# Residual turns by plain transposes, an unshared residual tail, an earlier start of each recurrence, and fewer GpSimd clears in a two-layer hybrid decoder step

## The chip, the cores and the metric

The kernel is one program on one core of a Trainium2 chip. The metric is device time in microseconds (us), lower is better. Three runs of the kernel before gave 1719.68, 1722.98 and 1724.67 us; the median, 1722.98 us, is the time before. A profile of one more execution gives the rows quoted below. The engines of a core are TensorE (PE in the rows, with PEld for its weight loads), VectorE (DVE), ScalarE (ACT), GpSimd (POOL) and the DMA queues, of which this kernel uses SyncE's (SP).

## What is computed

A prompt of 1024 tokens and eight short samples (8 x 4 tokens) go through two layers of width 1024: a sliding-window attention layer and a gated DeltaNet layer. Cut to what matters here:

```python
for layer in range(2):
    h, gate = modulate(x, c, norm_g[layer], w_mod[layer], b_mod[layer])   # rms_norm(x) * (1 + scale) + shift
    x = x + gate * branch(h)                                              # attention, then DeltaNet
y = rms_norm(x, final_norm_g)

def gated_delta_chunked(...):
    lower = where(strict, (kb @ k.T) * decay, 0)              # one system per chunk and head
    sol = triangular_solve(lower + eye, rhs)                  # unit lower triangular
    def step(S, xs):                                          # the recurrence over the chunks
        u = w_v - w_k @ S
        o = q_dec @ S + qk @ u
        S = S * g_tot + k_dec.T @ u
        return S, o
```

Between the layers each token row is scaled by its reciprocal root mean square, turned (tokens on partitions become features on partitions) and shifted and scaled, to be the moving operand of the second layer's projections.

## The kernel before

All matrix work is in float32 accuracy: a projection splits both operands into a high and a low float32r half and adds three products (`h2hi` by `wh`, `h2lo` by `wh`, `h2hi` by `wl`). The work runs in this order: modulation and the first layer's projections; attention; the first output projection with the residual and the turn into the second layer (about 425 to 570 us of the profile); the second layer's projections with the DeltaNet work woven in (about 540 to 1436 us); the second output projection with the samples' states and the final norm (to the end).

The order on each engine is not written out by hand. The big projections (`project`, lines 549 to 574) and output products (lines 1437 to 1469) are plain loops, and between any two of their matmuls `stages()` (line 497) asks a list of generators whether their next piece may be issued. A generator yields conditions: counters of other pieces, `ready(...)` and `idle(...)`, which compare a simple clock kept by `Core` with the time at which a tile is expected, and `bank(tag)`, which hands out PSUM banks. The numbers in `K` and `KR` rank the generators. So an edit of a condition or of an operation shifts everything behind it, on all engines. Each engine then executes its own list strictly in that order. Where a helper records an operation, the profile gives it line 89.

Residual tail. `rows_in` (1328) loads a 128-token row block of `x` into one of two `xt` tiles. `add_out` (1337) multiplies the output product by the gate into a tile `y` (two buffers), adds it to one half of `xt` on GpSimd and squares it on ScalarE; the second half (`hf` = 1) of block i waits until block i-1 has left `shape` (line 1341, counter `shaped`). `shape` (1376) takes the reciprocal root (`rsqrt`, eleven small VectorE operations), makes a diagonal matrix `dg` of it, which lies in one of the two `y` buffers, and multiplies: four float32 matmuls `dg` by `xt` in each of two halves (`kk`) scale and turn the block at once into a `lg` bank. Then `fu` is shifted and scaled from the bank, and split into `h2hi` and `h2lo`. Blocks are taken in the order 0, the samples, 1 to 7, so step i = 8 is block 7. Behind the last output products stand the conv weights' transpose `cwr`, copied by VectorE to `cT`, and the first projection of the second layer (`kw`).

DeltaNet. Per pair of heads `hq` (0 to 7), `solve` (1832) makes the systems in four tiles `UZ` (one for two chunks), and sends their 32x32 diagonal blocks out by DMA. `invert` (1882) fetches them as `X`, inverts them on VectorE, and before that clears the 16 diagonal strips of the `UZ` tiles on GpSimd (lines 1892 to 1896). `diagonal` multiplies each `UZ` tile by the inverted blocks `Xd` into `M`, and then overwrites the whole `UZ` tile with the transposed inverses; `blocks` fills the parts off the diagonal in six steps. `chain` (1985) is the recurrence over eight chunks; it waits until all four tiles of its head pair are solved (`st["ready"]` = 3 counts the solve as 2 and the scores `decayed` as 1). `gating` (1992) normalizes its output with a reciprocal root on GpSimd. After the last projection (`z15`) the program waits for the solve of `hq` = 7 (2175), closes its pools and opens those of the second output projection, whose rows `of` come by DMA.

Of the kernel before, what the change touches and what calls it, by code (L numbers as in the profile page):

```python
# [5 lines left out]
F32 = mybir.dt.float32  # L6
# [8 lines left out]
P = 128  # L15
# [204 lines left out]
def body(tc, I, O, cst_ap, dbg=None):  # L220
# [27 lines left out]
        z10 z11 k6 v5 q6 z12 z13 k7 v6 q7 v7 z14 z15""".split()]  # L248
    MM = (0, 20)
    ORDER = [("q", 2), ("q", 3), ("q", 4), ("q", 5), ("z", 0), ("k", 1), ("z", 1), ("z", 2), ("q", 6), ("q", 7),  # L250
             ("z", 3), ("z", 4), ("z", 5), ("z", 6), ("z", 7)]
# [269 lines left out]
    def ready(*ts):  # L521
        return lambda: plain() or nc.ready(ts) <= nc.free["tensor"]
# [789 lines left out]
    if True:  # L1312
# [15 lines left out]
        def rows_in(i, t):  # L1328
            yield lambda: shaped[0] >= i - 1
            xt = rows_[i] = x2.tile([P, D], F32, tag="xt", name="xt", bufs=2)  # L1330
            nc.sync.dma_start(xt[0:P if t < NB else TS], xp_rows[t * P:(t + 1) * P] if t < NB else xs_rows)
            if t == NB:
                o, w = COFF["sels"]
                selt = rows_["sel"] = xo.tile([P, w], F32, name="sels")
                nc.sync.dma_start(selt, cst_ap[:, o:o + w])

        def add_out(pj, i, t, hf):

            parts = P if t < NB else TS
            ns = slice(hf * 512, (hf + 1) * 512)  # L1340
            yield lambda: gathered[0] == 2 * i + hf and i in rows_ and shaped[0] >= i - 1 + hf
            xt = rows_[i][0:parts]
# [33 lines left out]
        def shape(i, t, xt, ss, parts):  # L1376
# [7 lines left out]
            rsqrt(nc, sm, rs, sv, 1, parts)  # L1384
            dg = x2.tile([P, 512], F32, tag="y", name="dg", bufs=2)[0:parts, 0:parts]
            nc.vector.tensor_scalar_mul(dg, ident[0:parts, 0:parts], rs)
            for kk in range(2):
                yield ready(dg, xt)
                pt = yield from bank("lg")
                for q in range(4):  # L1390
                    nc.tensor.matmul(pt[:, q * parts:(q + 1) * parts], xt[:, (4 * kk + q) * P:(4 * kk + q + 1) * P], dg,
                                     start=True, stop=True)
                fu = x2.tile([P, 4, P], F32, tag="fu", name="fu", bufs=2)
# [249 lines left out]
    if True:  # L1643
# [238 lines left out]
        def invert(hq, st, Ld, Xdd):  # L1882
# [8 lines left out]
            nc.gpsimd.memset(X.rearrange("p i c -> p (i c)")[:, 0:1024:33], 1.0)  # L1891
            for cp_ in range(4):
                uv = UZ[cp_].rearrange("p h c i -> p (h c) i")
                for b in range(4):
                    bs = slice(32 * b, 32 * b + 32)
                    nc.gpsimd.memset(uv[bs, :, bs], 0.0)
            yield soon(X)
# [38 lines left out]
            def blocks():  # L1936


                for v in range(6):
# [15 lines left out]
                    st["pairs"] = max(0, v - 1)  # L1955
                st["ready"] = st.get("ready", 0) + 2
                solved[0] += 1
# [4 lines left out]
        def decayed(hq, st):  # L1962
# [8 lines left out]
            for c4 in range(2):  # L1971
# [739 lines left out]
```

## Time and profile before

| | |
|---|---|
| median of three runs | 1722.98 us (1719.68 to 1724.67) |
| the profiled execution, its own time | 1721.68 us |
| its span in the profile | 1719.9 us |
| PE busy share, idle | 95%, 90.9 us |
| DVE, ACT, POOL busy share | 70%, 50%, 36% |
| mean granted TensorE clock | 0.981 |

How to read the rows: a row of the timeline has the start and the duration in us, then engine, line, operation, the tile written, `<-`, the tiles read, shapes, and `xN` for N instructions merged; a bracket says how long the engine had idled before it and which instruction ended that wait. A row of `windows` has the stretch, then the busy time of PE, PEld, DVE, ACT and POOL in it with instruction counts, the granted TensorE clock (1.00 is full speed), the DMA share and GB/s. A float32 matmul is two instructions in the timeline, a transpose one.

### The profile page before, as it was taken

What the parts mean: (1) busy time and instruction counts of PE and PEld (TensorE: products, weight loads), DVE (VectorE), ACT (ScalarE), POOL (GpSimd) and SP (SyncE); (2) the same over time, 40 slices, a digit from 0 to 9 for tenths busy, and PEclk for the clock granted to TensorE, in tenths of its full rate; (3) what the DMA queues carried; (4) which work ended last, traced back from release to release, by engine and by line L of the source; (5) the groups of instructions that cost most, each with busy time, mean ns of one, the idle gap of its engine ahead of it and who ended that gap; (6) DMA issues with size and microseconds to landing.
All of it is one profiled execution on the core that took longest, in us unless ns stands there. A gap on an engine that the chain in (4) does not pass through costs nothing.

```text
span 1719.9 us, 31798 instructions
## 1 busy us (share of the span) xinstructions
PE 1629.0 (95%) x10666; PEld 1436.5 (84%) x10666; DVE 1204.6 (70%) x3538; ACT 862.6 (50%) x2514; POOL 613.4 (36%) x1170
## 2 busy tenths in 40 slices
PE   6999999998999999999899999999999998999897
PEld 5988888986777898999889899899999896767685
DVE  4526676564565578897889878788797875468677
ACT  4625565444333546475463655654656654333332
POOL 2601111112112226463453534445344455323332
PEclk9999999999999999999999999999999999999999
DMA  9542221233243142232332324224242237765885
GB/s 331 150 138 66 59 58 50 56 89 111 86 134 105 54 111 50 66 97 56 106 74 66 98 52 112 64 72 114 51 115 60 51 85 209 236 181 160 255 259 171
DMA packets 281573, 191.78 MB, mean 112 GB/s; under 512 B 98361, under 2 KB 253881, under 8 KB 281378
## 3 DMA queue, kind: packets, MB, share of 16 engines
q1 hardware_dynamic: 281410, 189.75, 38.1%
q8 instruction: 85, 1.39, 0.3%
q14 instruction: 78, 0.64, 0.1%
HBM read 144.68 MB, written 47.04 MB: 111 GB/s over the span
## 4 chain that ended last, share of the span: by engine, by line
PE 30%; DVE 8%; DMA 4%; ACT 3%; issue 2%; POOL 2%; SPq 1%; POOLq 0%; ACTq 0%; DVEq 0%
PE ps_pj L89 17%; PE ps_lg L89 4%; PE ps_mi L89 4%; PE ps_tr L89 2%; PE ps_ob L89 2%; DMA S<-in_state_gdn_s 2%; DVE vT L89 1%; DVE UZ L89 1%; DMA out_new_s_s<-S 1%; POOL rst L89 1%; DMA out_y_p<-xt 1%; DVE rst L89 1%; DVE S L89 1%; SPq L89 1%; DVE tmp L89 0%
## 5 line engine op out<-in xcount | busy, mean ns | idle before, releaser
L89 PE MATMUL ps_pj<-h2hi,wl 128*128 128x384 f32 (+1 forms) x1128 | 383.1, 340 | 2.7 <-POOL wl L89 2.7
L89 PE MATMUL ps_pj<-h2hi,wh 128*128 128x384 f32 (+1 forms) x1128 | 383.2, 340 | 2.1 <-ACT wh L89 2.1
L89 PE MATMUL ps_pj<-h2lo,wh 128*128 128x384 f32 (+1 forms) x1128 | 381.6, 338 | 0.0
L89 POOL TENSOR_TENSOR wl<-wr,wh 128x512 fp32r<-128x512 f32 x122 | 163.4, 1340 | 543.3 <-ACT wh L89 492.9
L89 PEld LDWEIGHTS ps_pj<-h2hi,wl 128*128 128x128 f32 x1128 | 216.0, 191 | 6.8 <-POOL wl L89 3.6
L89 PEld LDWEIGHTS ps_pj<-h2hi,wh 128*128 128x128 f32 x1128 | 215.9, 191 | 4.8 <-ACT wh L89 2.4
L89 PEld LDWEIGHTS ps_pj<-h2lo,wh 128*128 128x128 f32 x1128 | 215.7, 191 | 3.3
L89 POOL TENSOR_TENSOR xt<-xt,y 128x512 f32<-128x512 f32 (+1 forms) x48 | 64.0, 1337 | 173.5 <-DVE y L89 138.1
L89 PE MATMUL ps_pj<-hlo,wh 128*128 128x384 f32 (+1 forms) x360 | 119.0, 331 | 0.0
L89 PE MATMUL ps_pj<-hhi,wh 128*128 128x384 f32 (+1 forms) x360 | 118.4, 329 | 0.0
L89 PE MATMUL ps_pj<-hhi,wl 128*128 128x384 f32 (+1 forms) x360 | 117.9, 328 | 0.0
L89 DVE SCALAR_TENSOR_TENSOR vT<-XR,cT,vT 128x384 f32<-128x384 f32 (+1 forms) x144 | 90.5, 638 | 25.4 <-ACT vT L89 23.8
L89 DVE TENSOR_TENSOR X<-X,tmp 64x31 f32<-64x31 f32 (+15 forms) x248 | 95.2, 384 | 8.5
L89 DVE TENSOR_TENSOR tmp<-X 64x31 f32<-64x31 f32 (+15 forms) x248 | 93.5, 377 | 4.9 <-POOL X L89 1.7
L89 ACT CAST wh<-wr 128x512 fp32r<-128x512 f32 x122 | 75.1, 616 | 13.1 <-PE ps_pj L89 8.0
L89 PEld LDWEIGHTS ps_pj<-hlo,wh 128*128 128x128 f32 x360 | 67.7, 188 | 11.2 <-issue 11.1
L89 ACT ACTIVATE vo<-vo,fo 128x128 f32<-128x128 f32 x128 | 42.2, 392 | 59.7 <-POOL fo L89 59.7
L89 PEld LDWEIGHTS ps_pj<-hhi,wh 128*128 128x128 f32 x360 | 67.7, 188 | 2.7 <-issue 2.7
L89 ACT ACTIVATE prob<-prob,nm 128x256 f32<-128x256 f32 (+1 forms) x128 | 62.2, 489 | 14.8 <-DVE nm L89 14.6
L89 PEld LDWEIGHTS ps_pj<-hhi,wl 128*128 128x128 f32 x360 | 67.7, 188 | 2.1 <-issue 2.1
L89 POOL TENSOR_TENSOR Xd<-Xc,cst 32x128 f32<-32x128 f32 x128 | 65.7, 513 | 10.7 <-DMA Xc<-Xdd 3.1
L89 ACT ACTIVATE qe<-ps_mi,Eg 128x128 f32<-128x128 f32 x112 | 35.0, 363 | 64.4 <-PE ps_mi L89 64.4
(580 smaller groups left out, 4235.0 us busy)
## 6 DMA issues: line engine op xcount, KB each, us to landing
wr<-in_gdn_w_in SPq DMA_DIRECT2D x96, 256.0 KB
S<-in_state_gdn_s SPq DMA_DIRECT2D x40, 256.0 KB
xt<-in_x_prompt SPq DMA_DIRECT2D x16, 512.0 KB
wm<-in_w_mod SPq DMA_DIRECT2D x16, 512.0 KB
wr<-in_swa_w_in SPq DMA_DIRECT2D x64, 128.0 KB
wmod<-in_w_mod SPq DMA_DIRECT2D x32, 256.0 KB
wm<-in_w_mod SPq DMA_DIRECT2D x32, 256.0 KB
DP<-gcr SPq DMA_DIRECT2D x64, 128.0 KB
```

Of the source, the lines that this page charges most:

```text
L89: inst = fn(*args, **kwargs)
```

## The change

Four edits.

1. `shape`: for the steps in `TP2` (0 to 7, all but the last) the diagonal product goes. Instead each half row of 512 columns is scaled into a new tile `xs`, by VectorE for the first half and ScalarE for the second (`TE2`), and turned by four transposes with the identity (`cst` in the rows).
2. `add_out`: the second half no longer waits for the block before to be shaped; `dg`, where it is still made, has a buffer of its own, not a `y` buffer. (`XT` = 2 leaves `rows_in` as it was.)
3. `chain` begins when the first of the four tiles is solved (`pairs` >= 1) and the scores are done, and waits for each further tile as it comes to it.
4. `invert` no longer clears the strips: 16 GpSimd memsets for each head pair, 128 in all.

```diff
+    TP2, TE2 = (0, 1, 2, 3, 4, 5, 6, 7), ('vector', 'scalar')
+    XT = 2
...
-            yield lambda: shaped[0] >= i - 1
-            xt = rows_[i] = x2.tile([P, D], F32, tag="xt", name="xt", bufs=2)
+            yield lambda: shaped[0] >= i - XT + 1
+            xt = rows_[i] = x2.tile([P, D], F32, tag="xt", name="xt", bufs=XT)
...
-            yield lambda: gathered[0] == 2 * i + hf and i in rows_ and shaped[0] >= i - 1 + hf
+            yield lambda: gathered[0] == 2 * i + hf and i in rows_
...
-            dg = x2.tile([P, 512], F32, tag="y", name="dg", bufs=2)[0:parts, 0:parts]
-            nc.vector.tensor_scalar_mul(dg, ident[0:parts, 0:parts], rs)
+            plain_ = i in TP2
+            if not plain_:
+                dg = x2.tile([P, P], F32, tag="dg", name="dg", bufs=2)[0:parts, 0:parts]
+                nc.vector.tensor_scalar_mul(dg, ident[0:parts, 0:parts], rs)
             for kk in range(2):
-                yield ready(dg, xt)
-                pt = yield from bank("lg")
-                for q in range(4):
-                    nc.tensor.matmul(pt[:, q * parts:(q + 1) * parts], xt[:, (4 * kk + q) * P:(4 * kk + q + 1) * P], dg,
-                                     start=True, stop=True)
+                if plain_:
+                    xs = x2.tile([P, 512], F32, tag="xs", name="xs", bufs=2)[0:parts]
+                    eng = TE2[kk]
+                    yield idle(eng, rs)
+                    if eng == "scalar":
+                        nc.scalar.activation(xs, xt[:, kk * 512:(kk + 1) * 512], AF.Copy, scale=rs)
+                    else:
+                        getattr(nc, eng).tensor_scalar_mul(xs, xt[:, kk * 512:(kk + 1) * 512], rs)
+                    yield ready(xs)
+                    pt = yield from bank("lg")
+                    for q in range(4):
+                        nc.tensor.transpose(pt[:, q * parts:(q + 1) * parts], xs[:, q * P:(q + 1) * P],
+                                            ident[0:parts, 0:parts])
+                else:
...
-            for cp_ in range(4):
-                uv = UZ[cp_].rearrange("p h c i -> p (h c) i")
-                for b in range(4):
-                    bs = slice(32 * b, 32 * b + 32)
-                    nc.gpsimd.memset(uv[bs, :, bs], 0.0)
...
-                st["ready"] = st.get("ready", 0) + 2
+                st["pairs"] = 4
...
-            st["ready"] = st.get("ready", 0) + 1
+            st["scored"] = True
...
-            yield lambda: st.get("ready", 0) == 3 and st.get("turned", 0) == 6 and finished[0] == hq - 1
+            yield lambda: st.get("pairs", 0) >= 1 and "scored" in st and st.get("turned", 0) == 6 and finished[0] == hq - 1
...
                 vt = vo[cp_]
+                yield lambda: st["pairs"] > cp_
                 pa, py = psb("mi"), psb("ob")
```

How the order on the engines moves, at three places. First TensorE at the end of the first output projection, where the turn of step i = 7 stands (`dg,xt` before, `cst,xs` in the change; `whi`, `wlo` are output products, `kw` the second layer's first projection). Before:

```order
L89 MATMUL ps_pj<-wlo,ohi 128x512
L89 MATMUL ps_pj<-h2hi,kw0h 128x384
L89 MATMUL ps_pj<-h2lo,kw0h 128x384
L89 MATMUL ps_pj<-h2hi,kw0l 128x384
L89 MATMUL ps_lg<-dg,xt 128x128 x4
L89 MATMUL ps_pj<-h2hi,kw0h 128x384
```

In the change:

```order
L89 MATMUL ps_pj<-whi,ohi 128x512
L89 MATMUL ps_pj<-whi,olo 128x512
L89 MATMUL ps_lg<-cst,cwr 128x128
L89 MATMUL ps_lg<-cst,xs 128x128 x4
L89 MATMUL ps_pj<-wlo,ohi 128x512
```

The turn moved from behind three `kw` matmuls to right behind the `cwr` transpose, ten output products and three projection matmuls earlier.

Second GpSimd where it prepares the solve of `hq` = 2 (`X` is the fetched blocks, `UZ` the strips, `rst` to `fo` the reciprocal root of a gating, `wl` the low halves of the weights that the next projection waits for). Before:

```order
L89 MEMSET X 64x32
L89 MEMSET UZ 32x4x32 x16
L89 TENSOR_TENSOR rst<-rsw 128x4
L89 TENSOR_TENSOR rst<-rst,mo 128x4
L89 TENSOR_SCALAR rst<-rst 128x4
L89 TENSOR_TENSOR rsw<-rst,rsw 128x4
```

In the change:

```order
L89 TENSOR_TENSOR fo<-rst,rsw 128x4
L89 MEMSET X 64x32
L89 TENSOR_TENSOR wl<-wr,wh 128x512 x2
L89 TENSOR_TENSOR rst<-rsw 128x4
```

Between the clear of `X` and the two weight splits stood 16 strip clears and a reciprocal root of twelve operations; both are gone from there, the clears altogether and the root to another place.

Third TensorE where the second layer's projections end (`UZ,M` are steps of `blocks` for `hq` = 7, `vo,UZ`, `us,ktok`, `uo,DP`, `S,kT` and `S,qT` the recurrence, `modG,selt` the gate rows, `h2hi,ohi` the first product of the second output projection). Before:

```order
L89 MATMUL ps_lg<-UZ,M 32x96 x4
L89 MATMUL ps_ob<-vo,UZ 128x128 x2
L89 MATMUL ps_mi<-us,ktok 128x256
L89 MATMUL ps_mi<-uo,DP 128x128 x2
L89 MATMUL ps_mi<-S,kT 128x256
L89 MATMUL ps_lg<-modG,selt 128x512 x2
L89 MATMUL ps_ob<-vo,UZ 128x128 x2
L89 MATMUL ps_pj<-h2hi,ohi 128x512
```

In the change:

```order
L89 MATMUL ps_lg<-UZ,M 32x96 x4
L89 MATMUL ps_mi<-us,ktok 128x256
L89 MATMUL ps_mi<-S,qT 128x256
L89 MATMUL ps_mi<-uo,DP 128x128 x2
L89 MATMUL ps_mi<-S,kT 128x256
L89 MATMUL ps_ob<-vo,UZ 128x128 x2
L89 MATMUL ps_lg<-modG,selt 128x512 x2
L89 MATMUL ps_mi<-us,ktok 128x256
L89 MATMUL ps_mi<-S,qT 128x256
L89 MATMUL ps_mi<-uo,DP 128x128 x2
L89 MATMUL ps_mi<-S,kT 128x256
L89 MATMUL ps_pj<-h2hi,ohi 128x512
```

The first chunk and half of the second now stand ahead of these rows, between the last projection matmuls, and the rest of the second and nearly all of the third stand in the stretch that held the first. For the other head pairs, the recurrence of `hq` = 0, 1 and 2 moves ahead by 44, 58 and 16 projection matmuls on the mean, that of 3 to 5 by at most one, and that of 6 moves back by 3 to 7.

More of the change, by code (lines that the diff above doesn't have):

```diff
@@ L1384, in shape @@
             rsqrt(nc, sm, rs, sv, 1, parts)
-            dg = x2.tile([P, 512], F32, tag="y", name="dg", bufs=2)[0:parts, 0:parts]
-            nc.vector.tensor_scalar_mul(dg, ident[0:parts, 0:parts], rs)
+            plain_ = i in TP2
+            if not plain_:
+                dg = x2.tile([P, P], F32, tag="dg", name="dg", bufs=2)[0:parts, 0:parts]
+                nc.vector.tensor_scalar_mul(dg, ident[0:parts, 0:parts], rs)
             for kk in range(2):
-                yield ready(dg, xt)
-                pt = yield from bank("lg")
-                for q in range(4):
-                    nc.tensor.matmul(pt[:, q * parts:(q + 1) * parts], xt[:, (4 * kk + q) * P:(4 * kk + q + 1) * P], dg,
-                                     start=True, stop=True)
+                if plain_:
[12 more added lines that the diff above has]
+                else:
+                    yield ready(dg, xt)
+                    pt = yield from bank("lg")
+                    for q in range(4):
+                        nc.tensor.matmul(pt[:, q * parts:(q + 1) * parts], xt[:, (4 * kk + q) * P:(4 * kk + q + 1) * P], dg,
+                                         start=True, stop=True)
                 fu = x2.tile([P, 4, P], F32, tag="fu", name="fu", bufs=2)
```

## The prediction

> **What bounds the kernel now.** I read the page's engine table first, then the busy time in stretches, then TensorE's list of waits, and last the timeline at the places that the change touches.
>
> ```profile
> PE 1629.0 (95%) x10666; PEld 1436.5 (84%) x10666; DVE 1204.6 (70%) x3538; ACT 862.6 (50%) x2514; POOL 613.4 (36%) x1170
> 440.00:480.00 40.00, 40.00 (x197) 30.59 (x196) 22.10 (x76) 13.22 (x32) 8.45 (x7) 1.00 0.29 99
> 720.00:760.00 40.00, 39.07 (x251) 37.03 (x250) 37.15 (x105) 25.92 (x87) 18.20 (x45) 1.00 0.34 95
> ```
>
> TensorE is the bound: 1629.0 of 1719.9 us, and in the residual stage (440 to 480) it never idles. So a term counts if it takes matmul time away from TensorE, or a wait of TensorE. VectorE comes close to it where the recurrences run (37.15 of 40 us), which matters for the rivals.
>
> The clock multiplies waits. Where TensorE has idled for more than about 2 us, the rows show a stretch of 3.4 or 6.8 us at half clock:
>
> ```profile
> 538.80:545.60 6.80, 6.04 (x22) 6.04 (x22) 1.40 (x3) 2.51 (x8) 2.73 (x5) 0.50 0.60 157
> 828.90:832.30 3.40, 3.33 (x12) 3.23 (x13) 2.31 (x4) 2.12 (x11) 1.26 (x2) 0.50 0.53 127
> 1443.30:1446.70 3.40, 3.40 (x7) 1.61 (x6) 1.30 (x3) 1.46 (x3) 0.00 (x0) 0.50 1.03 310
> ```
>
> A busy TensorE loses half of such a stretch: 3.4 us of the first, 1.7 us of the second.
>
> **Term (a), the plain turns: less TensorE work.** What a turn costs is read from the start of its group to the start of what follows, among matmuls that run back to back.
>
> ```profile
> 467.25 0.39 PE L89 MATMUL ps_mi<-whi,olo 128*128 128x512 f32 x1
> 467.48 0.39 PE L89 MATMUL ps_mi<-wlo,ohi 128*128 128x512 f32 x1
> 467.71 1.05 PE L89 MATMUL ps_lg<-dg,xt 128*128 128x128 f32 x8
> 468.52 0.48 PE L89 MATMUL ps_pj<-whi,ohi 128*128 128x512 f32 x1
> 453.27 1.07 PE L89 MATMUL ps_lg<-dg,xt 32*128 32x32 f32 x8
> 454.28 0.50 PE L89 MATMUL ps_mi<-whi,ohi 128*128 128x512 f32 x1
> 706.08 0.60 PE L89 MATMUL ps_lg<-cst,qT 128*128 128x128 f32 x4
> 706.44 0.42 PE L89 MATMUL ps_pj<-h2lo,wh 128*128 128x384 f32 x1
> ```
>
> The diagonal group takes 468.52 - 467.71 = 0.81 us, the samples' group 1.01 us, and four transposes of the same size, the nearest thing that the trace has, 706.44 - 706.08 = 0.36 us. Steps 0 to 7 are seven full blocks and the samples: 14 x (0.81 - 0.36) + 2 x (1.01 - 0.36) = 6.3 + 1.3 = 7.6 us. I take 7.5. Bounds: 0, if each transpose waits for its `xs` as long as it saves, and 7.6.
>
> What it adds is a scaling of 512 columns on each of two engines:
>
> ```profile
> L89 DVE TENSOR_SCALAR dg<-cst,rs x9: 228/287/1600, 436.3 to 559.6; 128x128 f32<-128x128 f32 x8, 32x32 f32<-32x32 f32 x1
> L89 DVE TENSOR_SCALAR prob<-prob,sm x128: 276/348/1427, 120.8 to 372.0; 128x256 f32<-128x256 f32 x112, 128x128 f32<-128x128 f32 x16
> L89 ACT ACTIVATE y<-xt x18: 622/632/643, 430.8 to 556.1; 128x512 f32<-128x512 f32 x16, 32x512 f32<-32x512 f32 x2
> ```
>
> VectorE: 287 ns at 128 columns and 348 at 256 are 61 ns for each 128, so 512 columns are about 0.47 us by extrapolation (an estimate; not under 0.35, and up to 1.4 to 1.6 us as the slowest of these rows). Eight of them less eight `dg` are 8 x (0.47 - 0.29) = 1.4 us. ScalarE: 8 x 0.63 = 5.0 us. Both are spread over some 100 us in which VectorE is busy 22.10 of 40 and ScalarE 13.22, and the order puts output products between scaling and turn. This cover goes where VectorE runs late; there each turn costs TensorE the delay.
>
> A rule of the Trainium skill speaks against this edit (TensorE: Matmul & The Clock Gate, Part 4: PE-mode transpose): transposes don't count as busy for the clock gate. By it the turns could bring half clock; that is a rival below.
>
> **Term (b), the wait at the tail.** Step i = 7 is where TensorE stands still.
>
> ```profile
> 529.41 0.69 DVE L89 TENSOR_TENSOR y<-ps_mi,gp 128x512 f32<-128x512 f32 x1
> 534.88 1.18 DVE L89 SCALAR_TENSOR_TENSOR rst<-rst,sv 128x1 f32<-128x1 f32 x1
> 536.10 1.19 DVE L89 SCALAR_TENSOR_TENSOR rsw<-rst,rsw 128x1 f32<-128x1 f32 x1
> 537.91 1.60 DVE L89 TENSOR_SCALAR dg<-cst,rs 128x128 f32<-128x128 f32 x1
> 537.88 1.27 POOL L89 TENSOR_TENSOR wl<-wr,wh 128x512 fp32r<-128x512 f32 x1 [0.53 <-ACT wh L89]
> 535.32 0.33 PE L89 MATMUL ps_pj<-h2hi,kw0h 128*128 128x384 f32 x1
> 539.56 2.08 PE L89 MATMUL ps_lg<-dg,xt 128*128 128x128 f32 x8 [3.01 <-DVE cT L89]
> ```
>
> The wait is put down to `cT`, but `dg`, just ahead of it on VectorE, ended at 537.91 + 1.60 = 539.51, so the root and `dg` were late. Their chain began with the gate product at 529.41, the first half's; the second followed it. Both were held back until the step before was shaped, and on the way three small operations took over 1 us each while GpSimd split weights. In the change the second doesn't wait. Its bank was complete 48 products of 0.23 us (rows of term a) ahead of the output products' end at 535.3, and about 1 us more for the modulation group among them: at about 523. So the chain can start some 5 us earlier; the turn itself stands 13 matmuls, some 2.8 us, earlier, and three VectorE operations of the length of `y` (0.69 us each) now stand ahead of `xs`. That leaves the data about level with the need, and I leave 0.7 us of the wait, one such operation: 3.01 - 0.7 = 2.3 us gained, and with it the half-clock stretch from 538.8 to 545.6, 3.4 us. Together 5.7 us; bounds 0 (the wait stays) and 6.4.
>
> The Trainium skill puts the limit higher (the same page, HAM oscillation: idle gaps of over about 3.4 us throttle). By that this gap of 3.01 us and the one of 2.38 us in (c) would cost no clock, and the sum would be 5.1 us smaller. This trace doesn't agree: both gaps stand right ahead of the first two stretches at 0.50 above, and the measurement decides.
>
> **Term (c), no strip clears.** 128 memsets of about 0.2 us are 25 us of GpSimd, which has time to spare. They cost something where weights queue behind them:
>
> ```profile
> 819.79 0.16 POOL L89 MEMSET X<- 64x32 f32 x1 [8.18 <-DMA X<-Ld]
> 819.85 3.83 POOL L89 MEMSET UZ<- 32x128 f32 x16
> 827.65 2.51 POOL L89 TENSOR_TENSOR wl<-wr,wh 128x512 fp32r<-128x512 f32 x2
> 828.98 0.69 PE L89 MATMUL ps_pj<-h2hi,wl 128*128 128x384 f32 x1 [2.38 <-POOL wl L89]
> ```
>
> Behind the fetch of `X`, the clears (3.83 us) and a root (3.9 us) hold `wl`, and TensorE waits 2.38 us and then loses 1.7 to half clock. In the change `wl` follows the clear of `X` at once, so with an equal fetch it is 7 us earlier: 4.1 us gained. Bounds: 0, if the fetch itself comes later, and 4.1. The other clears hold up nothing that TensorE waits for.
>
> **Term (d), the start of the recurrences.** It moves TensorE work and removes none, so only waits count. The last head pair's first chunks have them, where the projections end:
>
> ```profile
> 1439.10 0.70 PE L89 MATMUL ps_mi<-us,ktok 128*128 128x256 f32 x2 [0.70 <-DVE us L89]
> 1441.52 0.71 PE L89 MATMUL ps_mi<-uo,DP 128*128 128x128 f32 x4 [1.72 <-ACT uo L89]
> 1451.67 0.60 PE L89 MATMUL ps_mi<-uo,DP 128*128 128x128 f32 x3 [2.17 <-ACT uo L89]
> 1439.70 0.43 SPq L89 DMA_DIRECT2D of<-gTd  x1
> 1444.48 0.62 ACT L89 CAST ohi<-of 128x512 fp32r<-128x512 f32 x1 [2.50 <-DMA of<-gTd]
> ```
>
> The first output product can't come before the rows `of`, fetched only after the last projection, are here and split: the bare stretch stays, whatever fills it. In the change the first chunk hides among projection matmuls, but the second and third stand bare in its place. So I count the wait of 2.17 us, whose chunk leaves the output stage, and nothing for the others: 2.0 us; bounds 0 and their sum, 4.6. The added wait for a solved tile is in the order only; on TensorE it puts block steps and projection matmuls between the chunks. Pairs 3 to 6 gain nothing; for 0 to 2 see the rivals.
>
> **The sum.** 7.5 + 5.7 + 4.1 + 2.0 = 19.3 us. Against it I set 2.0 us of new waits, two of the eight VectorE scalings stretched by 1.0 us as the small operations above were. The profiled execution took 1721.7 us (1719.9 in the span, 1.8 around it): 1721.7 - 17.3 = 1704.4. It was 1.3 us faster than the median of the runs, so I say 1705, 1.0% below that median.
>
> **The rivals.**
>
> *Only the matmul time goes.* The chain at the tail is still late by 2 us or more, so half clock stays, and the fetch of `X` holds `wl` as before: (a) and some of (d), about 9 us, 1712 to 1714. For it: (b) and (c) each rest on one wait, and the orders around them are dealt anew.
>
> *More waits go.* The recurrences of pairs 0 to 2 move ahead by 16 to 58 projection matmuls, 3 to 10 us, and the waits around them are dealt anew:
>
> ```profile
> PE ps_tr L89 <- ACT vT L89: 8.7, 6, 3.9
> PE ps_mi L89 <- ACT uo L89: 3.9, 2, 2.4
> PE ps_tr L89 <- ACT vo L89: 3.3, 2, 3.1
> ```
>
> These are 15.9 us in 600 to 1436; with half clock behind the longest three (3.9, 3.1, 2.4 us, 1.7 each at least) up to 21. If half goes without a successor, about 1694.
>
> *Nothing comes of it.* All 16 turns wait for their `xs` by what they save (0.45 us), and the tail's wait stays: about 1719. Against it: the order keeps output products between scaling and turn.
>
> *Slower: early recurrences against VectorE.* Place: 640 to 760, where VectorE is busy 37.15 of 40 us. Recurrence operations that now come 8 to 10 us earlier stand in its queue ahead of the taps of `vT` and `kT`, and TensorE waits for these as in the `vT` row. Price: one wait of 3.9 us with its 1.7 us of half clock is 5.6; four of them, 22 us, eat the sum, and from the fifth it is slower than the bound; with six, 1704 + 34 = 1738. For it: VectorE is nearly full there. Against it: it is the same work, only spread differently.
>
> *Slower: turns that don't hold the clock.* Were transposes idle time to the gate, each of the 16 turns could bring a stretch of half clock: 16 x 1.7 = 27 us, 1704 + 27 = 1731; from eleven of them on it is slower. The attention stage speaks against it:
>
> ```profile
> 120.00:360.00 240.00, 238.56 (x1629) 208.40 (x1627) 158.93 (x596) 132.99 (x444) 31.28 (x24) 1.00 0.22 60
> L89 PE MATMUL ps_mi<-cst,prob x240: 270/272/331, 122.4 to 372.7; 128*128 128x128 f32 x120
> ```
>
> 240 transposes stand there in groups of four and eight between matmuls, and the clock is 1.00 throughout. This is the rule of the Trainium skill named in (a); the trace doesn't bear it out for such short groups.
>
> **How the numbers follow.** My forecast 0.48 (1699 to 1709), only the matmul time 0.22, more waits 0.12, nothing 0.09, slower by early recurrences 0.07, by the clock 0.02. A measurement of this kernel can tell about 0.3%, 5.2 us, from no change. Faster by more than that means below 1717.8: 0.48 + 0.22 + 0.12 = 0.82. Within it: 0.09 and a little of the slower cases, 0.10. Slower: 0.08. The range takes in the sum with its bounds and the first two rivals, 1690 to 1720; the slower cases and the edges of the others, under 2 in 10, stay out.
>
> **What would show it.** (a): `xs` turns of about 0.36 us from start to start, and more than 6 us less between the first `modG,sels` product and the first `kw` matmul. (b): no TensorE wait over 1 us around `cwr`, and clock 1.00 there. (c): no `MEMSET UZ` on GpSimd, and no TensorE wait for `wl`. (d): the two `uo` waits gone or under 1 us. The rivals: waits for `xs` in TensorE's list, new waits of over 2 us for `vT`, `kT` or `vo` between 600 and 900, or stretches at 0.50 inside the residual stage. Most likely to make me wrong is a new wait of over 2 us, since each brings its half-clock stretch along.

## The result, and the profile after

| | before | after |
|---|---|---|
| median (range, runs) | 1721.39 us (1719.68 to 1724.67, 4) | 1702.16 us (1699.97 to 1704.92, 4) |
| ratio, 95% interval | | 0.9891 [0.9873, 0.9909] |
| both timed again, six and more runs | 1716.40 us | 1700.79 us, 0.9905 [0.9877, 0.9934] |
| the profiled execution, its span | 1721.68, 1719.9 us | 1704.92, 1703.1 us |
| TensorE busy, idle in the span | 1629.0, 90.9 us | 1618.1, 85.0 us |

Forecast were 1705 us in all and 1704.4 us for the profiled execution. The sum was right. The runs below bear out (a) and (b) in the residual stage, (a) only together with (b); of (c) the wait goes but little time with it, and (d) gains nothing.

Where the time went is read by stages. First the engine table of the changed kernel's page:

```profile
PE 1618.1 (95%) x10602; PEld 1423.8 (84%) x10602; DVE 1204.8 (71%) x3538; ACT 866.4 (51%) x2522; POOL 587.4 (34%) x1042
```

TensorE's busy time fell by 10.9 us, and its idle time by 5.9. Then its busy time by stage; a row has the stretch, its length, then busy time of PE, PEld, DVE, ACT, POOL, the granted clock, DMA share and GB/s. The stretches run from the first `modG,sels` product to the last `kw0h` product (residual stage), to the last `h2hi,wl` product (projections), to the end (output stage).

```profile
436.75:561.45 124.70, 123.06 (x631) 98.47 (x631) 80.35 (x232) 58.81 (x131) 28.88 (x25) 1.00 0.35 108
561.45:1414.93 853.48, 826.37 (x5834) 778.99 (x5833) 698.43 (x1939) 489.56 (x1519) 381.54 (x826) 0.99 0.30 82
1414.93:1703.10 288.17, 256.15 (x1213) 191.51 (x1211) 179.59 (x532) 96.67 (x237) 90.24 (x115) 0.95 0.69 209
```

The same stretches of the kernel before:

```profile
437.27:575.27 138.00, 133.64 (x694) 109.22 (x693) 77.65 (x225) 52.56 (x119) 27.92 (x25) 0.98 0.31 98
575.27:1434.69 859.42, 827.86 (x5802) 780.75 (x5801) 697.52 (x1933) 489.65 (x1518) 407.04 (x952) 0.98 0.30 80
1434.69:1719.90 285.21, 254.91 (x1245) 191.66 (x1243) 184.82 (x544) 98.73 (x240) 91.66 (x117) 0.96 0.71 213
```

The reader is to see that 13.3 us come from the residual stage and 5.9 from the projections, and that the output stage gave 3.0 back (in a second execution of the changed kernel it took 282.7 us, so no gain or loss is shown there). In the residual stage TensorE idles 1.6 us where it idled 4.4, at full clock.

A plain turn in the changed kernel, in the timeline of TensorE:

```profile
481.47 0.60 PE L89 MATMUL ps_lg<-cst,xs 128*128 128x128 f32 x4
481.82 0.48 PE L89 MATMUL ps_mi<-wlo,ohi 128*128 128x512 f32 x1
```

and the scalings in the view of tile `xs`, where the three numbers are the shortest, median and longest in ns:

```profile
L89 DVE TENSOR_SCALAR xs<-xt,rs x8: 465/478/487, 438.4 to 525.2; 128x512 f32<-128x512 f32 x7, 32x512 f32<-32x512 f32 x1
L89 ACT ACTIVATE xs<-xt,rs x8: 705/718/741, 443.6 to 535.3; 128x512 f32<-128x512 f32 x7, 32x512 f32<-32x512 f32 x1
```

A turn takes 481.82 - 481.47 = 0.35 us (0.36 were taken), VectorE's scaling 0.478 us (0.47), ScalarE's 0.718 (0.63).

The tail of the residual in the changed kernel, in TensorE's timeline:

```profile
526.29 0.60 PE L89 MATMUL ps_lg<-cst,xs 128*128 128x128 f32 x4
526.64 0.48 PE L89 MATMUL ps_pj<-wlo,ohi 128*128 128x512 f32 x1
...
536.04 0.66 PE L89 MATMUL ps_lg<-cst,xs 128*128 128x128 f32 x4 [1.35 <-ACT xs L89]
```

and in busy times and clock from 536 to 542 us:

```profile
536.00:542.00 6.00, 5.96 (x36) 4.89 (x37) 4.59 (x16) 1.45 (x3) 0.00 (x0) 1.00 0.51 143
```

The first half of step 7 is turned without a wait; the second waits 1.35 us for ScalarE's scaling, and the clock stays at 1.00. The wait of 3.01 us and its half-clock stretch are gone.

Where the recurrence of the last pair meets the second output projection, the changed kernel has a new wait. `qk` and `zq` are the samples' queries and keys, `qk` fetched by DMA and copied by VectorE into `zq`; `ohi` and `olo` are the high and low halves of the product's first rows `of`. Timeline rows of TensorE, ScalarE and VectorE:

```profile
1423.31 0.47 PE L89 MATMUL ps_pj<-h2hi,ohi 128*128 128x512 f32 x1
1428.04 0.79 PE L89 MATMUL ps_pj<-h2hi,olo 128*128 128x512 f32 x1 [4.26 <-DVE olo L89]
...
1422.58 0.64 ACT L89 CAST ohi<-of 128x512 fp32r<-128x512 f32 x1
...
1426.45 0.93 DVE L89 COPY zq<-qk 128x64 f32<-128x64 f32 x4 [3.88 <-POOL fo L89]
1427.30 0.68 DVE L89 TENSOR_TENSOR olo<-of,ohi 128x512 fp32r<-128x512 f32 x1
```

`ohi` was ready at 1423.2, but `olo` stood on VectorE behind copies that waited 3.88 us, for the fetch of `qk`. (The row names GpSimd's `fo`, which isn't read there; in the experiment on this wait, below, the row of the same copy names the fetch.)

### The profile page after: what moved, and what is told of

The parts are those of the page before. It is cut to its first block, busy times and chain, and to the rows that moved or that the text cites. A ratio compares the mean times of both kernels' runs of the same rounds, so it can differ in the third digit from the quotient of the medians.

```text
span 1703.1 us, 31539 instructions
## 1 busy us (share of the span) xinstructions
PE 1618.1 (95%) x10602; PEld 1423.8 (84%) x10602; DVE 1204.8 (71%) x3538; ACT 866.4 (51%) x2522; POOL 587.4 (34%) x1042
## 5 line engine op out<-in xcount | busy, mean ns | idle before, releaser
L89 ACT CAST wh<-wr 128x512 fp32r<-128x512 f32 x122 | 75.1, 616 | 13.7 <-PE ps_pj L89 10.9
L89 PEld LDWEIGHTS ps_pj<-hlo,wh 128*128 128x128 f32 x360 | 67.8, 188 | 11.2 <-issue 11.1
L89 ACT COPY XR<-ps_pj 128x384 f32<-128x384 f32 (+1 forms) x96 | 43.1, 449 | 54.4 <-PE ps_pj L89 54.0
```

Source lines behind the costliest of these rows:

```text
L89: inst = fn(*args, **kwargs)
```

## The experiments

First each edit alone on the kernel before, then each one taken back from the changed kernel, then two places by themselves. Ratios are to the kernel before on the same chip, with 95% intervals. Stage lengths of one profiled execution each, in us, by the marks above:

| kernel | residual | projections | output | ratio |
|---|---|---|---|---|
| before | 138.0 | 859.4 | 285.2 | 1 |
| turns alone | 144.6 | 854.5 | 298.0 | 1.0122 [1.0098, 1.0146] |
| loose second half alone | 130.1 | 857.2 | 291.5 | 0.9983 [0.9965, 1.0000] |
| no clears alone | 135.6 | 855.1 | 289.7 | 1.0003 [0.9984, 1.0022] |
| early start alone | 136.8 | 889.4 | 281.5 | 1.0183 [1.0157, 1.0208] |
| early start, last pair alone | 134.0 | 860.5 | 283.0 | 1.0008 [0.9985, 1.0030] |
| changed | 124.7, 124.2 | 853.5, 852.8 | 288.1, 282.7 | 0.9905 [0.9877, 0.9934] |
| changed, turns by `dg` | 129.6 | 852.0 | 279.7 | 0.9923 [0.9898, 0.9947] |
| changed, second half held back | 145.9 | 852.9 | 293.3 | 1.0076 [1.0052, 1.0100] |
| changed, clears back | 124.1 | 855.8 | 291.0 | 0.9945 [0.9923, 0.9966] |
| changed, late start | 123.9 | 886.5 | 294.0 | 1.0092 [1.0062, 1.0121] |

Kernels with the same residual stage show how far one execution can be trusted: the four with that of before give 134.0 to 138.0, the five with that of the change 123.6 to 124.7 (the fifth is the kernel of the `olo` wait below). The output stage scatters by 5 us between executions of the changed kernel.

**The turns alone**

```diff
+    TP2, TE2 = (0, 1, 2, 3, 4, 5, 6, 7), ('vector', 'scalar')
...
-            dg = x2.tile([P, 512], F32, tag="y", name="dg", bufs=2)[0:parts, 0:parts]
-            nc.vector.tensor_scalar_mul(dg, ident[0:parts, 0:parts], rs)
+            plain_ = i in TP2
...
+                    for q in range(4):
+                        nc.tensor.transpose(pt[:, q * parts:(q + 1) * parts], xs[:, q * P:(q + 1) * P],
+                                            ident[0:parts, 0:parts])
```

> The kernel before with the plain turns alone (the second half of a block still waits for the block before to be shaped, and clears and the start of the recurrence are as before). Theory of the sum: from the first modG,sels product to the first kw matmul TensorE takes 98.0 us in the kernel before and about 92 us here (14 groups at 0.36 in place of 0.81 us); the wait at the turn of step 7 stays over 1 us, because its second half is still held back. In all about -7.5 us, 1714. Rival (the scalings come late and each turn waits for what it saves): 97 to 98 us for the same stretch, waits for xs in TensorE's list, 1719 to 1722. Second rival (the new places of everything behind the stage decide): the stretch is 92 us, but the time lies 4 us or more from 1714, by waits between 600 and 1440 us.

Measured: 1738.17 us against 1718.30, 20 us slower; none of the three theories. TensorE's timeline at its tail:

```profile
516.12 0.60 PE L89 MATMUL ps_lg<-cst,xs 128*128 128x128 f32 x4
...
536.46 1.11 PE L89 MATMUL ps_lg<-cst,xs 128*128 128x128 f32 x4 [5.12 <-DVE xs L89]
539.95 0.58 PE L89 MATMUL ps_lg<-h2hi,wab 128*64 128x384 f32 x1 [2.37 <-POOL wab L89]
...
558.42 0.66 PE L89 MATMUL ps_lg<-cst,xs 128*128 128x128 f32 x4 [2.87 <-ACT xs L89]
```

and a stretch of its busy times:

```profile
541.20:544.60 3.40, 3.40 (x12) 2.34 (x11) 0.00 (x0) 0.00 (x0) 0.00 (x0) 0.50 0.55 159
```

(`wab` are the weights of a small projection of the second layer.) The turn at 516.12 is that of step 5, at 536.46 that of step 6. With the second half held back, the steps form a loop: a block's second half waits for the block before to be shaped, its root waits for the second half, and its shaping for the root. A plain turn puts a scaling on each of two queues into that loop. Steps 2 to 5 are turned at 472.06, 487.62, 501.86 and 516.12 here, 14.7 us apart, at 467.71, 481.97, 495.44 and 508.90 before, 13.7 apart, and at 463.90, 476.60, 488.08 and 500.12 in the changed kernel, 12.1 apart. With the second half loose and `dg` (the kernel of the loose second half alone, below) they are 13.0 apart: held back, the plain turns lengthen a step by 1.0 us, loose, they shorten it by 0.9. So before the output products end this kernel is a step behind, TensorE has nothing left, and it waits 5.12, 2.37 and 2.87 us, with half clock behind. The output stage, too, was longer here, by 13 us in this execution, with a different order; that part isn't traced to one cause.

**The second half held back again, turns plain**

```diff
-            yield lambda: gathered[0] == 2 * i + hf and i in rows_
+            yield lambda: gathered[0] == 2 * i + hf and i in rows_ and shaped[0] >= i - 1 + hf
```

> The changed kernel with the second half of a block waiting again until the block before is shaped. Theory (the two edits of the residual stage belong together: with plain turns and the second half held back, the root starts later and its scaling stands between it and the turn): waits for xs of over 3 us around 530 to 560 us and half clock there, as with the plain turns alone (5.12 and 2.87 us); by the last kw0h matmul at least 12 us behind the changed kernel; 1714 or more. Rival (the sum of single terms): 5.7 us behind, 1708.

Measured: 1731.47 us, 15 above the kernel before, and some 21 us more in the residual stage than the changed kernel. Its list of waits between 430 and 580 us:

```profile
PE ps_lg L89 <- DVE xs L89: 5.6, 2, 5.1
PE ps_lg L89 <- ACT xs L89: 2.9, 1, 2.9
PE ps_lg L89 <- POOL wab L89: 2.4, 1, 2.4
```

The waits of the turns alone are back, in another kernel. The theory holds: the first two edits belong together.

**The loose second half alone**

```diff
-            yield lambda: gathered[0] == 2 * i + hf and i in rows_ and shaped[0] >= i - 1 + hf
+            yield lambda: gathered[0] == 2 * i + hf and i in rows_
...
-            dg = x2.tile([P, 512], F32, tag="y", name="dg", bufs=2)[0:parts, 0:parts]
+            dg = x2.tile([P, P], F32, tag="dg", name="dg", bufs=2)[0:parts, 0:parts]
```

> The kernel before with the loosened second half and dg in a buffer of its own, the turns still products with the diagonal. Theory: the stretch from the first modG,sels product to the first kw matmul stays at about 98 us, the wait of 3.01 us at the turn of step 7 falls below 1 us, and the clock there is 1.00: -5.7 us, 1715 to 1716. Rival (the chain of the root is late anyway): a wait of over 2 us stays with its stretch at 0.50, and the time is 1719 to 1722.

Measured: 1715.74 us, 2.6 us faster by the medians, and a residual stage of 130.1 us, 6.0 below the mean of the four that have that of before (136.1). The four differ by the tail: its wait was 3.01, 1.70, 2.95 and 1.70 us (before, no clears, early start, early start for the last pair), and half clock took 3.4, 1.7, 1.7 and 0 us of the stage. So against single executions the gain is 3.9 to 7.9 us. No wait over 1 us is left in the tail:

```profile
530.00:575.00 45.00, 43.97 (x275) 40.18 (x275) 28.71 (x71) 24.51 (x51) 12.17 (x17) 1.00 0.27 71
```

From the first `modG,sels` product to the first `kw` matmul it is 100.0 us, not 98: more work stands ahead of that mark. In the stage the theory holds; in all less was gained. The order behind the stage is new, too, and what was lost there isn't traced.

**The plain turns' own price**

```diff
-    TP2, TE2 = (0, 1, 2, 3, 4, 5, 6, 7), ('vector', 'scalar')
+    TP2, TE2 = (), ('vector', 'scalar')
```

> The changed kernel with all turns as products with the diagonal again. The order of everything behind the residual stage is the same as in the changed kernel, so this is the price of the plain turns by itself. Theory (term a): +7.6 us from the first modG,sels product to the first kw matmul, less the wait of 1.35 us for xs at 536 us, which goes: +6.2 us in all, 1708. Rival (VectorE's and ScalarE's scalings cost back what the turns save): within 2 us of 1702.

Measured: 1704.33 us, ratio 0.9923 against 0.9905 and 0.9891 of the changed kernel: 3 to 5.5 us slower, the intervals overlapping in part. The residual stage tells more: from the first `modG,sels` product to the first `kw` matmul 99.95 us here and 92.28 in the changed kernel, 7.67 us, and over the whole stage 129.6 against 124.1 (the mean of five executions), 5.5 us. (The order within the stage is not quite the same: sixteen turns stand ahead of that mark here, fifteen in the changed kernel, and a plain turn is 0.35 us.) So the turns save about what was worked out, and the tail takes some 2 us of it back: over the stage TensorE idles 0.20 us here and 1.64 in the changed kernel, 1.35 of it the wait for ScalarE's scaling; the rest isn't traced.

**No clears alone**

```diff
-            for cp_ in range(4):
-                uv = UZ[cp_].rearrange("p h c i -> p (h c) i")
-                for b in range(4):
-                    bs = slice(32 * b, 32 * b + 32)
-                    nc.gpsimd.memset(uv[bs, :, bs], 0.0)
```

> The kernel before without the GpSimd clears, and nothing else. Theory: the wait of 2.38 us for wl at 829 us and the half clock behind it go, -4.1 us, 1717. Rival (the wait moves to the next thing on GpSimd or to a later fetch, or other waits come with the new order): no wl wait, but within 2 us of the kernel before, 1719 to 1723.

Measured: 1718.74 against 1718.30 us over 12 runs: no difference. In the profiled execution the wait for `wl` had gone and the projections were 4.3 us shorter, as worked out, but the output stage, whose order differs too, was 4.5 us longer, about its scatter. For the whole it is the rival's case.

**The clears put back into the changed kernel**

```diff
             nc.gpsimd.memset(X.rearrange("p i c -> p (i c)")[:, 0:1024:33], 1.0)
+            for cp_ in range(4):
...
+                    nc.gpsimd.memset(uv[bs, :, bs], 0.0)
```

> The changed kernel with the GpSimd clears back. Until the third pair of heads TensorE's order is the changed kernel's, behind it that of other kernels. Theory (term c, the clears hold weight splits): a wait of TensorE for wl of 2 us or more between 800 and 850 us with half clock behind it, +4 us, 1706. Rival 1 (the order decides, the clears only as they change it): no wait for wl over 1 us, and the time lies 6 us or more from the changed kernel's, 1708 to 1735. Rival 2 (the clears cost nothing here): within 2 us of it.

Measured: 1707.08 against 1700.79 us on the same chip, 6.3 us slower. GpSimd's rows and TensorE's wait in this kernel:

```profile
814.61 0.16 POOL L89 MEMSET X<- 64x32 f32 x1 [4.46 <-DMA X<-Ld]
814.68 3.86 POOL L89 MEMSET UZ<- 32x128 f32 x16
818.62 2.67 POOL L89 TENSOR_TENSOR wl<-wr,wh 128x512 fp32r<-128x512 f32 x2
...
820.00 0.69 PE L89 MATMUL ps_pj<-h2hi,wl 128*128 128x384 f32 x1 [3.80 <-POOL wl L89]
```

and the same place in the changed kernel:

```profile
817.67 0.15 POOL L89 MEMSET X<- 64x32 f32 x1 [4.40 <-DMA X<-Ld]
817.79 1.29 POOL L89 TENSOR_TENSOR wl<-wr,wh 128x512 fp32r<-128x512 f32 x1
```

With the clears, `wl` starts 4.0 us after the clear of `X`, without them 0.1 us, and TensorE's wait is as long as the clears. Yet hardly any of the 6.3 us is this wait. Up to about 1008 us every engine has the same order in both kernels, the clears apart. From the last `kw0h` product to the last TensorE product of this common order it takes 447.0 us with the clears, and 446.6 and 445.8 in two executions without them: 0.4 to 1.2 us, less than the 1.7 us of one half-clock stretch. Two things eat the gain. Without the clears TensorE waits 1.62 us for `vo` soon behind this place, with a stretch of 3.4 us at half clock (rows in the last section); with them it doesn't. And one pair of heads earlier, the next weight split takes the place of the clears beside a VectorE operation on `qT`. With the clears:

```profile
680.20 3.78 POOL L89 MEMSET UZ<- 32x128 f32 x16
680.72 0.61 DVE L89 SCALAR_TENSOR_TENSOR qT<-XR,cT,qT 128x384 f32<-128x384 f32 x1
682.77 0.68 PE L89 MATMUL ps_mi<-uo,DP 128*128 128x128 f32 x4 [0.57 <-DVE UZ L89]
```

In the changed kernel:

```profile
681.19 1.27 POOL L89 TENSOR_TENSOR wl<-wr,wh 128x512 fp32r<-128x512 f32 x1 [0.64 <-ACT wh L89]
681.24 1.64 DVE L89 SCALAR_TENSOR_TENSOR qT<-XR,cT,qT 128x384 f32<-128x384 f32 x1
684.33 0.68 PE L89 MATMUL ps_mi<-uo,DP 128*128 128x128 f32 x4 [1.60 <-DVE UZ L89]
```

The same `qT` operation took 0.61 us beside the clears and 1.64 beside the split; the copy of `UZ` is queued behind it, TensorE waits 1.60 us in place of 0.57, and the clock is at 0.50 from 686.4 to 689.8, where it is 1.00 with the clears. The rest of the 6.3 us lies behind 1008 us, where the orders differ.

**The early start alone, and the late start in the changed kernel**

```diff
-            yield lambda: st.get("ready", 0) == 3 and st.get("turned", 0) == 6 and finished[0] == hq - 1
+            yield lambda: st.get("pairs", 0) >= 1 and "scored" in st and st.get("turned", 0) == 6 and finished[0] == hq - 1
...
+                yield lambda: st["pairs"] > cp_
```

> The kernel before with the earlier start of the recurrence alone. Theory: TensorE work of the first chunks moves between projection matmuls, the uo wait of 2.17 us at the second output projection's start goes, -2.0 us, 1719. Rival A (early recurrences run into a full VectorE between 640 and 760 us): new waits of over 2 us for vT or vo there, 1724 or more. Rival B (a bigger gain by waits among 600 and 1440): 1715 or less.

The second kernel has the same lines the other way round, in the changed kernel.

> The changed kernel with the recurrence waiting for all four solved tiles again, as in the kernel before. The early start alone on the kernel before took 1749 us, 31 us more. Theory 1 (the early start itself costs that, and the other edits hide it): about 1672 here. Theory 2 (what costs is the order that the rest of the program falls into; from the third pair of heads on this kernel's TensorE order is that of the early start alone): over 1720 here, with TensorE's waits between 850 and 1430 us at about 30 us, as there, against 16 in the changed kernel. Theory of the prediction (the early start is worth about 2 us): 1704 to 1706.

Measured: 1749.22 us with the early start alone, 31 us slower than before, and 1732.86 us without it in the changed kernel, some 32 us slower than that (1.0092 against 0.9905). The edit costs 31 us where it is made alone, and taking it back costs as much. So it is not the start by itself. Both kernels have nearly the same TensorE order from the third pair of heads on: its recurrence stands 55 projection matmuls later than in the kernel before in both, the solve of the seventh pair 59 later. Busy times from 850 to 1420 us, in the early start alone:

```profile
850.00:1420.00 570.00, 541.04 (x3779) 506.32 (x3778) 463.95 (x1262) 318.81 (x1001) 257.27 (x621) 0.99 0.27 73
```

in the changed kernel with the late start:

```profile
850.00:1420.00 570.00, 537.43 (x3739) 502.73 (x3737) 453.71 (x1247) 317.56 (x1011) 236.31 (x553) 0.99 0.27 74
```

and in the changed kernel:

```profile
850.00:1420.00 570.00, 557.80 (x4012) 524.05 (x4011) 469.01 (x1304) 335.16 (x1043) 260.39 (x586) 1.00 0.31 82
```

TensorE idles 29.0 and 32.6 us against 12.2 (17.4 in the kernel before). Over the whole of the projections it idles 51.5 and 50.2 us, against 27.1 in the changed kernel and 31.6 before: some 20 us of the 31 are waits, and the rest isn't traced. VectorE isn't fuller in the slow ones, so it is not a full engine that holds TensorE up. The idle time is spread; the two longest groups of waits of the early start alone in that stretch:

```profile
PE ps_tr L89 <- ACT vT L89: 7.0, 7, 2.4
PE ps_tr L89 <- ACT XR L89: 3.2, 2, 2.4
```

Theory 2 holds: the order into which the rest falls is worth 30 us, more than any edit here. Which of its moves matters most stays open.

**The early start for the last pair alone**

```diff
-            yield lambda: st.get("ready", 0) == 3 and st.get("turned", 0) == 6 and finished[0] == hq - 1
+            yield lambda: st.get("pairs", 0) >= (1 if hq == HQ - 1 else 4) and "scored" in st and st.get("turned", 0) == 6 and finished[0] == hq - 1
```

> The kernel before with the early start for the last pair of heads alone, so that TensorE's order changes only where the projections end. Theory (term d as it was worked out): the wait of 2.17 us for uo goes, -2.0 us, with the bounds 0 and -4.6, 1714 to 1718 where the kernel before takes 1718. Rival (the early start costs by itself, as in its run alone): 1722 or more.

Measured: 1718.07 against 1716.40 us, 1.0008 [0.9985, 1.0030]: nothing. Its only wait of over 0.5 us between 1425 and 1460 us:

```profile
PE ps_pj L89 <- DVE olo L89: 4.1, 1, 4.1
```

and the longest group of the kernel before between 1430 and 1460:

```profile
PE ps_mi L89 <- ACT uo L89: 3.9, 2, 2.2
```

The waits for `uo` go, as worked out, and one for `olo` of the same length comes.

**The `olo` wait**

```diff
+                yield lambda: len(prepared.get(0, ())) > 0
                 yield idle("vector", qk)
                 nc.vector.tensor_copy(zq[:, b, :, c0:c0 + 8].rearrange("p h (i t) -> p h i t", i=2),
```

> The changed kernel with VectorE's copies zq<-qk placed behind its first olo split at the start of the second output projection. Theory (in the changed kernel olo, whose input is ready at about 1423.2 us, stands behind zq copies that wait for the transfer of qk until 1426.4): TensorE's wait of 4.26 us at 1428 falls below 1 us and the half clock behind it, 6.8 us long, goes: -6 to -7 us, 1695 to 1697. Rival (another piece of the same start is late next, the rows of or the state S): the wait only changes its name, 1700 to 1703.

Measured: 1699.99 us, 0.9895 [0.9872, 0.9919]: the changed kernel's time. The wait changed its name, the rival's case. ScalarE, VectorE and TensorE in its timeline:

```profile
1426.52 0.62 ACT L89 CAST ohi<-of 128x512 fp32r<-128x512 f32 x1 [4.84 <-DMA of<-gTd]
...
1427.69 1.34 DVE L89 TENSOR_TENSOR h2lo<-wr,h2hi 128x512 fp32r<-128x512 f32 x1 [3.32 <-ACT h2hi L89]
1428.95 0.60 DVE L89 TENSOR_SCALAR us<-ps_ob,sd 128x128 f32<-128x128 f32 x2
...
1429.61 0.79 PE L89 MATMUL ps_mi<-us,ktok 128*128 128x256 f32 x1 [4.58 <-DVE us L89]
```

The copies no longer hold `olo` (the first of them, at 1422.14, waited 1.39 us for `qk<-smd`). Now ScalarE stands 4.84 us at the fetch of the next rows `of`, the weight cast `h2hi` is queued behind it, VectorE's `h2lo` waits for that, and `us` is queued behind `h2lo`. The start of this projection waits for transfers, whichever of them is named.

**Both places together.** The changed kernel once more, and with step 7's turn by `dg` and the `zq` copies behind `olo`:

```diff
-    TP2, TE2 = (0, 1, 2, 3, 4, 5, 6, 7), ('vector', 'scalar')
+    TP2, TE2 = (0, 1, 2, 3, 4, 5, 6), ('vector', 'scalar')
...
+                yield lambda: len(prepared.get(0, ())) > 0
```

> The changed kernel again, timed on the same chip as the three others of this call. 1.1% below the kernel before, as in its first timing.

> The changed kernel with step 7's turn as a product with the diagonal again and the zq copies behind the first olo split; the order behind both places is the changed kernel's. Theory: the wait for ScalarE's xs (1.35 us) goes against 0.9 us more of TensorE time, and the start of the second output projection wins up to 2 us: 1 to 4 us below the changed kernel. Rival (both places are bound by something else): within 1 us of it.

Measured: 1700.79 us (0.9905) and 1700.31 us (0.9901 [0.9872, 0.9930]). The second had no wait for `xs` left, and took as long. No version here beats the changed kernel by more than the measurement can tell.

## Why the prediction was right, point by point

- **(a), 7.5 us: right in size.** 7.67 us to the first `kw` matmul against the kernel with `dg`, 0.35 us a turn. Over the whole stage 5.5 us stay, and 7.5 - 2.0 = 5.5 were forecast, but that the two agree is luck. The 2.0 us stood for VectorE scalings stretched by 1.0 us, and none of the eight was (465 to 487 ns); what came was 1.4 us more of idle time, most of it the wait for a ScalarE scaling. Against the kernel before, the sign of "more than 6 us less" to the first `kw` matmul was missed (98.05 to 92.28, 5.8 us): fourteen turns stood ahead of that mark before, fifteen do in the changed kernel. The term's lower bound, 0, was wrong for the edit alone: with the second half held back the turns cost 8.5 us of the stage (144.6 against 136.1), through the loop of steps. The prediction bounded the scalings' delay turn by turn and did not follow it from step to step.
- **(b), 5.7 us: right.** 6.0 us with the edit alone, against a mean; the term was read from one execution, the one of the four with the longest wait and the most half clock. The chain of the root started in time, as worked out, and 1.00 was granted there. Of the wait 0.7 us were to be left; 0.5 to 1.35 us are, over five executions, so "no TensorE wait over 1 us around `cwr`" was missed in the profiled one.
- **(c), 4.1 us: right about the wait, wrong about its worth.** 3.80 us of wait come back with the clears. But the term counted nothing that follows: a wait of 1.62 us for `vo`, with its half clock, takes the place. And "The other clears hold up nothing that TensorE waits for" left out what runs in their stead: one pair earlier it is a weight split, beside which a VectorE operation took 1.64 us in place of 0.61, and TensorE waits for what is queued behind it. Up to 1008 us 0.4 to 1.2 us of gain are left. Alone the edit gained 4.3 us in the projections and nothing in all.
- **(d), 2.0 us: wrong.** "So I count the wait of 2.17 us, whose chunk leaves the output stage": the chunk left and the wait went, but what stands bare there is not the recurrence, it is the start of the output projection, which waits for transfers; 4.26 us for `olo` came instead (3.72 in a second execution). With the last pair alone nothing is gained. The prediction had said of that stretch that it stays bare "whatever fills it", and then counted one of its waits all the same.
- **The rivals.** "Early recurrences against VectorE" was priced at 1738, and the early start alone took 1749, but not for that reason: in the rival's place, 640 to 760 us, TensorE idles 5.7 us with the early start alone and 4.8 before; most of the loss lies behind 850 us, VectorE is not fuller there, and a kernel without the early start has it too. The other slower case could not come about here: the residual stage of the changed kernel runs at 1.00, but a turn is 0.35 us, and by the counts of the last section idle time of that size brings no half clock, so the stage doesn't test whether turns hold the clock. Other stretches of these runs do. From 100 us on, the 14 profiles have 25 cells of the grid described there in which TensorE waits for 1.08 to 1.67 us and turns tiles (mostly `prob`) for another 0.4 to 1.1 us, over 2.0 us together. Four of them were followed by half clock, all four with 1.59 us or more of waits alone; cells with 2.0 us or more of waits always were. So transposes don't count as idle time there. The Trainium skill's rule that transposes don't count as busy for the clock gate (TensorE: Matmul & The Clock Gate, Part 4: PE-mode transpose) is not borne out by these cells.

So the total came out to 0.2% with (d) at 0 in place of 2.0 and (c) at about 1 in place of 4.1. What made up for them are the residual stage, 13.3 us shorter where 7.5 + 5.7 - 2.0 = 11.2 were forecast, and the projections, 5.9 us shorter, of which the clears account for about 1 us up to 1008 us; the rest isn't traced to one cause, and came with a new order. That order could as well have cost 30 us, and no term of the prediction stood for it. That it did not was not foreseen but lucky.

## What to carry to other kernels

An edit that shortens a link and one that loosens the loop in which the link lies should be judged together: alone the first can lose (here 8.5 us of its stage, 20 in all) where both together win (12 us of the stage). A wait that goes is worth only what doesn't come in its place: compare the two kernels up to the last point to which their orders agree. Where a planner sets the order, make each edit alone and take each one back: if both cost the same, it is the order that is measured and not the edit. And a wait at the start of a stage that waits for its transfers goes only when the transfers come earlier.

## What the hardware showed unexpectedly

The granted clock changes on a fixed grid. In each of the 14 profiles the stretches at 0.50 start whole multiples of 3.413 us apart (in the changed kernel 8, 57, 76, 89, 131 and 306 steps behind the first). What counts is how long TensorE idles within one cell of that grid, not how long a gap is. Two waits of the changed kernel in TensorE's timeline:

```profile
828.54 1.20 PE L89 MATMUL ps_tr<-cst,vo 128*128 128x128 f32 x4 [1.62 <-ACT vo L89]
...
858.11 0.55 PE L89 MATMUL ps_tr<-cst,vT 128*128 128x128 f32 x3 [2.13 <-ACT vT L89]
```

and the cells around them in busy times, two for the first and three for the second:

```profile
826.40:829.80 3.40, 1.78 (x10) 1.08 (x10) 3.12 (x9) 1.65 (x5) 1.36 (x4) 0.99 0.08 29
829.80:833.20 3.40, 3.40 (x16) 3.40 (x15) 3.30 (x6) 0.62 (x1) 1.28 (x1) 0.51 0.37 135
853.70:857.10 3.40, 2.28 (x18) 2.05 (x16) 2.79 (x9) 3.34 (x8) 1.86 (x3) 1.00 0.01 2
857.10:860.50 3.40, 2.03 (x14) 1.79 (x14) 2.72 (x9) 3.31 (x15) 0.00 (x0) 1.00 0.03 5
860.50:863.90 3.40, 2.51 (x19) 2.26 (x20) 2.86 (x9) 3.34 (x13) 0.47 (x1) 1.00 0.35 77
```

A wait of 1.62 us inside one cell brings half clock in the next; one of 2.13 us that lies across two brings none. Over the 14 profiles, from 430 us to the last matmul, the cells at full clock were counted by TensorE's idle time in them: with under 1.3 us one of 4861 was followed by half clock (at 1.20 us), with 1.3 to 1.7 us 10 of 69, with 1.7 to 2.0 us 17 of 28, with 2.0 us or more all 90. (The ends of matmuls are modelled in the profile, so these bounds are rough.) So the limit lies near half a cell, and a gap between 1.7 and 3.4 us costs clock or not by where it falls. The prediction's "more than about 2 us" was a fair mean of this. The Trainium skill has the window, 3413 ns and free-running (TensorE: Matmul & The Clock Gate, Part 1: The HAM clock gate), and the trace agrees; its limit for gaps of about 3.4 us (the same page, HAM oscillation) is not what these runs show.
